# Forward substitution of 64x64 blocks on VectorE: spreading a finished row instead of gathering the rows above

## Chip, cores and metric

The kernel runs on one core of one Trainium2 chip. The metric is the device time of one execution in microseconds (us). The kernel before was run three times: 2924.29 us is the median, 2923.99 and 2924.81 the ends.

## The reference, cut to what matters

One inference step of a one-layer hybrid decoder over 1024 prompt positions and 32 sample positions: a SwiGLU feed-forward block, a layer norm, one wide projection that feeds two mixers in parallel (a gated spatial MLP and a gated DeltaNet), a merge, a layer norm, and a second feed-forward block. The DeltaNet mixer works in chunks of 64 positions with 8 heads. For each chunk and head it needs the inverse of a unit lower triangular 64x64 matrix:

```python
a_mat = jnp.where(strict, jnp.einsum('nbhid,nbhjd->nbhij', kb, k) * decay, 0.0)
eye = jnp.eye(L, dtype=q.dtype)
t_inv = lax.linalg.triangular_solve(eye + a_mat, jnp.broadcast_to(eye, a_mat.shape),
                                    left_side=True, lower=True, unit_diagonal=True)
u_vals = jnp.einsum('nbhij,nbhjv->nbhiv', t_inv, v * beta[..., None])
w_vals = jnp.einsum('nbhij,nbhjd->nbhid', t_inv, kb * jnp.exp(G)[..., None])
```

The prompt has 16 chunks and 8 heads, so there are 128 such matrices: one on each of the 128 partitions.

## The kernel before

TensorE does the large products in float32 split into a high and a low part, three matmuls for each product, in "unit pieces": `unit_piece` makes one 128x352 output from 8 weight tiles, 24 matmuls (lines 387 to 389). There are three pieces, one for each third of the positions, for each 128 columns of a weight. Everything else (convolutions, norms, DeltaNet, sampling) is a Python generator in a "lane".

The order of the instructions is laid out by a planner inside the kernel while it is built. It keeps `self.pet`, the time at which TensorE would be, and for VectorE, ScalarE and GpSimd an `Engine` object (line 151) that charges each instruction a fixed part plus a part for each element of a partition: 0.10 us and 1.04 ns on VectorE (`Core`, line 174), 0.12 us and 2.2 ns on GpSimd. A charge begins at the later of the engine's own planned end and `cur`, the planned end of the instruction issued just before in the same lane step, whichever engine that was on. `tick` runs after each three matmuls of a piece and lets each lane that is due go on by one step (line 335). `drain(g)` (line 356) lets planned time run until generator `g` is finished; no matmul of a unit piece is issued during a drain. `tt` (line 304) puts an elementwise instruction on GpSimd or VectorE, whichever would end first by the plan, with a bonus for GpSimd. Each engine then executes its own instructions in the order in which they were issued.

The work around the change is in `mixer` (line 1718). Unit pieces for k, q and v run first; their convolutions and transposes are generators that use VectorE heavily. `solve_gen` (line 1243) begins when all eight heads of k are done. It loads A, the 128 negated strictly lower triangular matrices, into `sA` (64x64 on each partition, row i and column j), and sets `sT` to the identity, held as `T[c, i]`: column c first, so that one column of the inverse is contiguous. For each row i from 1 to 63 it multiplies the columns found so far by row i of A (`prod`, tile `sP` or `sQ`) and sums over the inner index (`fold`, a tensor_reduce) into `T[:, i]`. Columns go in groups of 16, which leaves out much of the zero triangle. For i over 32 one of the products goes to GpSimd where the plan has it free. After each step, `ahead()` holds the generator as long as VectorE's planned end is over 0.8 us ahead of TensorE.

When the solve is done, four ScalarE copies write the transposed inverse back into `sA`, and two DMAs on SyncE's queue write `sT` and `sA` to memory. `comb_gen` (line 1295), eight in one lane, loads parts of them for each head and combines two 64x64 blocks into a 128x128 block with the `px` matmuls.

Beside the solve, in order of issue, there are z pieces, four units of gate pieces ("ga"), and two `sample_gen` (line 1448), one after the other in one lane. A sample generator has a chain of small steps over TensorE, VectorE and ScalarE, and ends with four rounds in which `spread` (line 1575) makes a tile `km`, TensorE makes 8 products `su` from it, and VectorE adds these to the states `s`. Line 1815 drains the second one, then adds the eight `comb_gen`. The gv pieces and further gate pieces follow, then lines 1843 to 1845 drain the solve, the spatial gate's norm (`gvln_gen`, lane "ln") and the last `comb_gen`, before the u pieces.

Of the kernel before, what the change touches and what calls it, by code (L numbers as in the profile page):

```python
# [12 lines left out]
F32 = mybir.dt.float32  # L13
# [3 lines left out]
ALU = mybir.AluOpType  # L17
AX = mybir.AxisListType
# [3 lines left out]
P = 128  # L22
# [239 lines left out]
class Kern:  # L262
# [979 lines left out]

    def solve_gen(self):

        nc = self.nc
        v = nc.vector
        while self.kdone < 8:
            yield 1.0
        yield 4.0
        Ab, Tb = self.big("sA", 4096), self.big("sT", 4096)  # L1250
        nc.sync.dma_start(Ab, self.scNd.rearrange("h s n i j -> (h s n) (i j)"))
        nc.gpsimd.memset(Tb, 0.0)
        nc.gpsimd.memset(Tb[:, 0:4096:65], 1.0)
        A, T = Ab.rearrange("p (i j) -> p i j", j=64), Tb.rearrange("p (c j) -> p c j", j=64)
        yield 8.0
        cost = 0.0
        m0, m1 = self.row("sP", F32, 1024), self.row("sQ", F32, 1024)

        def prod(e, i, c0, o, m):
            n, w = min(16, i - c0), i - c0  # L1260
            x = m[:, o:o + n * w].rearrange("p (c j) -> p c j", j=w)
            e.tensor_tensor(out=x, in0=T[:, c0:c0 + n, c0:i], in1=A[:, i, c0:i].unsqueeze(1).to_broadcast([P, n, w]), op=ALU.mult)
            return c0, n, x

        def fold(i, c0, n, x):
            v.tensor_reduce(out=T[:, c0:c0 + n, i:i + 1].rearrange("p c j -> p (c j)"), in_=x, axis=AX.X, op=ALU.add)
        def ahead():
            return v.end > self.pet + 0.8
        for i in range(1, 64):
            b1 = prod(nc.gpsimd if i > 32 and nc.gpsimd.end < self.pet + 0.3 else v, i, 16, 0, m1) if i > 16 else None  # L1270
            b0 = prod(v, i, 0, 0, m0)
            while ahead():
                yield -1.0
            fold(i, *b0)
            while ahead():
                yield -1.0
            late = [prod(v, i, c0, o, m0) for c0, o in ((32, 0), (48, 512)) if i > c0]
            while ahead():
                yield -1.0
            for b in late:  # L1280
                fold(i, *b)
            while ahead():
                yield -1.0
            if b1:
                fold(i, *b1)
            while ahead():
                yield -1.0
        for s in range(4):
            nc.scalar.copy(A[:, s * 16:(s + 1) * 16, :], T[:, :, s * 16:(s + 1) * 16].rearrange("p c j -> p j c"))
            yield  # L1290
        nc.sync.dma_start(self.scT, Tb)
        nc.sync.dma_start(self.scTn, Ab)
        self.solved = True
# [905 lines left out]
```

## Time and profile before

| | before |
| --- | --- |
| median of three runs | 2924.29 us |
| profiled execution | 2927.93 us |
| its span, first to last instruction | 2926.2 us |
| TensorE busy | 2763.6 us, 94% of the span |
| VectorE busy | 1811.3 us, 62% |
| ScalarE busy | 1111.8 us, 38% |
| GpSimd busy | 1473.4 us, 50% |
| mean granted TensorE clock | 0.970 of full speed |

The engines are named PE (TensorE matmuls), PEld (its weight loads), DVE (VectorE), ACT (ScalarE), POOL (GpSimd) and SP (SyncE). Nearly all elementwise instructions are recorded under line 167, the call in `Engine`, so they are told apart by the names of their tiles. Matmuls are pipelined: a busy share of PE near 100% does not say that it is at its peak, and a granted clock under 1.00 stretches the same matmuls. Idle time is put down to what ended it.

### The profile page before, as it was taken

The page shows a single profiled execution, that of the slowest core. Times are in us where ns is not written, and L with a number is a line of the kernel's source. Part 1 is how long each engine was busy: PE and PEld are TensorE (multiplying, and loading weights), DVE is VectorE, ACT ScalarE, POOL GpSimd, SP SyncE. Part 2 cuts the span into 40 slices and gives each one's busy share as a digit, 9 for nine tenths or more (in the row PEclk, how much of TensorE's full clock was granted, in tenths as well). Part 3 has the DMA queues.
Part 4 walks back from the last instruction along what each step waited for, and adds up shares of the span by engine and source line. Part 5 has one row for each costly group of instructions (what it writes and reads, how often), then busy time and mean ns, then how long its engine had stood idle before and what let it go on. Part 6 is the DMA issues. An engine that isn't in the chain of part 4 may idle for free.

```text
span 2926.2 us, 44704 instructions
## 1 busy us (share of the span) xinstructions
PE 2763.6 (94%) x17467; PEld 2716.2 (93%) x17467; DVE 1811.3 (62%) x2859; ACT 1111.8 (38%) x2216; POOL 1473.4 (50%) x867
## 2 busy tenths in 40 slices
PE   9998999999899998998999999999989989999995
PEld 8998899999789998998999999999989988999995
DVE  4646655455768999999363445036785466554556
ACT  4433333333345654321632433224443333333332
POOL 6656866665435452445233123232466568666653
PEclk9999999999899999998999999999999999999997
DMA  6442222221238995442444278475333422212211
GB/s 232 138 144 87 92 65 66 87 75 56 74 92 155 204 189 118 119 137 77 130 131 159 86 250 280 142 258 191 126 116 133 140 84 93 73 62 83 80 51 40
DMA packets 236867, 359.41 MB, mean 123 GB/s; under 512 B 72144, under 2 KB 169040, under 8 KB 236272
## 3 DMA queue, kind: packets, MB, share of 16 engines
q1 hardware_dynamic: 236656, 356.55, 40.1%
q8 instruction: 137, 2.24, 0.3%
q14 instruction: 74, 0.61, 0.1%
HBM read 279.59 MB, written 76.91 MB: 122 GB/s over the span
## 4 chain that ended last, share of the span: by engine, by line
PE 67%; DVE 17%; issue 6%; POOL 5%; ACT 2%; DMA 2%; SPq 0%; POOLq 0%; DVEq 0%; ACTq 0%
PE ps L387 16%; PE ps L389 15%; PE ps L388 15%; PE A L387 3%; PE A L389 3%; PE A L388 3%; DVE v L167 2%; DVE k L167 2%; DVE m L167 1%; POOL s L167 1%; PE F L387 1%; PE F L389 1%; PE F L388 1%; DVE q L167 1%; POOL wl L167 1%
## 5 line engine op out<-in xcount | busy, mean ns | idle before, releaser
L167 POOL TENSOR_TENSOR wl<-w,wh 128x1024 fp32r<-128x1024 f32 x217 | 546.6, 2529 | 768.9 <-ACT wh L167 591.2
L387 PE MATMUL ps<-x1h,wh 128*128 128x352 f32 x1536 | 515.2, 335 | 1.8 <-ACT wh L167 1.1
L389 PE MATMUL ps<-x1h,wl 128*128 128x352 f32 x1536 | 497.4, 324 | 1.8 <-POOL wl L167 1.8
L388 PE MATMUL ps<-x1l,wh 128*128 128x352 f32 x1536 | 497.9, 324 | 0.0
L387 PE MATMUL ps<-h,wh 128*128 128x352 f32 x1056 | 344.7, 326 | 18.3 <-DVE m L167 9.0
L389 PE MATMUL ps<-h,wl 128*128 128x352 f32 x1056 | 343.4, 325 | 6.5 <-POOL wl L167 6.5
L167 POOL TENSOR_TENSOR s<-w,s 128x512 fp32r<-128x512 f32 x158 | 217.7, 1390 | 194.8 <-ACT s L167 194.1
L387 PEld LDWEIGHTS ps<-x1h,wh 128*128 128x128 f32 x1536 | 293.3, 191 | 6.8 <-issue 1.4
L389 PEld LDWEIGHTS ps<-x1h,wl 128*128 128x128 f32 x1536 | 292.4, 190 | 2.1 <-POOL wl L167 2.1
L388 PEld LDWEIGHTS ps<-x1l,wh 128*128 128x128 f32 x1536 | 293.7, 191 | 0.1
L167 ACT CAST wh<-w 128x1024 fp32r<-128x1024 f32 (+1 forms) x257 | 263.6, 1044 | 75.7 <-PE ps L388 45.1
L388 PE MATMUL ps<-h,wh 128*128 128x352 f32 x704 | 228.0, 324 | 1.0 <-DVE h L167 1.0
L387 PEld LDWEIGHTS ps<-h,wh 128*128 128x128 f32 x1056 | 199.6, 189 | 20.9 <-DVE m L167 9.9
L389 PEld LDWEIGHTS ps<-h,wl 128*128 128x128 f32 x1056 | 200.0, 189 | 8.0 <-POOL wl L167 7.9
L167 ACT CAST s<-w 128x512 fp32r<-128x512 f32 x220 | 130.9, 618 | 167.7 <-DVE w L167 69.9
L387 PE MATMUL A<-T,s 128*128 128x352 f32 x528 | 176.7, 335 | 17.3 <-ACT T L167 10.6
L388 PE MATMUL A<-T,s 128*128 128x352 f32 x528 | 173.7, 329 | 0.5 <-DVE T L167 0.5
L389 PE MATMUL A<-T,s 128*128 128x352 f32 x528 | 173.5, 329 | 0.0
L167 DVE TENSOR_TENSOR p<-p,B 128x352 f32<-128x352 f32 x44 | 22.8, 519 | 235.0 <-PE B L389 235.0
L167 DVE SCALAR_TENSOR_TENSOR m<-ps,m 128x352 f32<-128x352 f32 x264 | 125.5, 515 | 32.6 <-PE ps L389 32.3
L167 DVE SCALAR_TENSOR_TENSOR acc<-ps,acc 128x352 f32<-128x352 f32 x264 | 125.7, 515 | 31.9 <-PE ps L389 31.6
L388 PEld LDWEIGHTS ps<-h,wh 128*128 128x128 f32 x704 | 132.9, 189 | 1.5 <-DVE h L167 1.5
(481 smaller groups left out, 7293.2 us busy)
## 6 DMA issues: line engine op xcount, KB each, us to landing
w<-in_wu SPq DMA_DIRECT2D x176, 512.0 KB
w<-in_wd SPq DMA_DIRECT2D x88, 512.0 KB
w<-in_wm SPq DMA_DIRECT2D x64, 512.0 KB
w<-in_wo SPq DMA_DIRECT2D x24, 512.0 KB
acc<-in_xt SPq DMA_DIRECT2D x12, 352.0 KB
scr_x<-acc SPq DMA_DIRECT2D x12, 352.0 KB
scr_z<-z SPq DMA_DIRECT2D x24, 176.0 KB
scr_ga<-tg SPq DMA_DIRECT2D x24, 176.0 KB
```

What stands on the lines that cost most here:

```text
L167: return f(*a, **kw)
L387: nc.tensor.matmul(ps[:, :C], lh, xh, start=(start and i == 0), stop=False, skip_group_check=not start)
L388: nc.tensor.matmul(ps[:, :C], lh, xl, start=False, stop=False, skip_group_check=not start)
L389: nc.tensor.matmul(ps[:, :C], ll, xh, start=False, stop=(i == n - 1), skip_group_check=not start)
```

## The change

For each j from 0 to 62, row j of the inverse is finished; it is multiplied by column j of A below the diagonal, for all columns c up to j and all rows i below j in one instruction, and a second instruction adds the products onto `T`. So 63 pairs of VectorE instructions take the place of the products and folds. No part goes to GpSimd, tile `sQ` is gone, and the planner is asked only once for each j, after the pair, whether VectorE is too far ahead. The work before the loop (load, memsets) and behind it (four copies, two stores) is the same.

```diff
-        cost = 0.0
-        m0, m1 = self.row("sP", F32, 1024), self.row("sQ", F32, 1024)
-
-        def prod(e, i, c0, o, m):
-            n, w = min(16, i - c0), i - c0
-            x = m[:, o:o + n * w].rearrange("p (c j) -> p c j", j=w)
-            e.tensor_tensor(out=x, in0=T[:, c0:c0 + n, c0:i], in1=A[:, i, c0:i].unsqueeze(1).to_broadcast([P, n, w]), op=ALU.mult)
-            return c0, n, x
-
-        def fold(i, c0, n, x):
-            v.tensor_reduce(out=T[:, c0:c0 + n, i:i + 1].rearrange("p c j -> p (c j)"), in_=x, axis=AX.X, op=ALU.add)
-        def ahead():
-            return v.end > self.pet + 0.8
-        for i in range(1, 64):
-            b1 = prod(nc.gpsimd if i > 32 and nc.gpsimd.end < self.pet + 0.3 else v, i, 16, 0, m1) if i > 16 else None
-            b0 = prod(v, i, 0, 0, m0)
-            while ahead():
-                yield -1.0
-            fold(i, *b0)
...
-            late = [prod(v, i, c0, o, m0) for c0, o in ((32, 0), (48, 512)) if i > c0]
...
-            for b in late:
-                fold(i, *b)
...
-            if b1:
-                fold(i, *b1)
-            while ahead():
+        m = self.row("sP", F32, 1024)
+        for j in range(63):
+
+            n, w = j + 1, 63 - j
+            x = m[:, 0:n * w].rearrange("p (c i) -> p c i", i=w)
+            t = T[:, 0:n, j + 1:64]
+            v.tensor_tensor(out=x, in0=T[:, 0:n, j:j + 1].to_broadcast([P, n, w]), in1=A[:, j + 1:64, j].unsqueeze(1).to_broadcast([P, n, w]),
+                            op=ALU.mult)
+            v.tensor_tensor(out=t, in0=t, in1=x, op=ALU.add)
+            while v.end > self.pet + 0.8:
                 yield -1.0
```

## Rows read from the trace of the kernel before

**Rows 1.** The page of the profile: busy time of DVE and PE in 40 equal slices of the span (73 us each), in tenths.

```profile
PE   9998999999899998998999999999989989999995
DVE  4646655455768999999363445036785466554556
```

**Rows 2.** Busy time of each engine in five stretches around the solve. Columns: stretch in us, its length, then PE, PEld, DVE, ACT and POOL busy us (instructions), granted PE clock, DMA share, GB/s.

```profile
1060.00:1190.00 130.00, 114.55 (x710) 113.08 (x709) 127.81 (x192) 57.86 (x125) 44.83 (x17) 0.92 0.65 122
1190.00:1345.00 155.00, 154.20 (x1037) 145.31 (x1037) 142.65 (x289) 43.15 (x103) 74.49 (x61) 1.00 0.35 118
1345.00:1405.00 60.00, 50.49 (x288) 49.13 (x286) 56.92 (x101) 16.63 (x44) 28.55 (x12) 0.80 0.21 71
1420.00:1435.00 15.00, 10.25 (x63) 9.78 (x62) 2.83 (x6) 6.87 (x19) 2.86 (x2) 0.77 0.57 176
1540.00:1560.00 20.00, 16.68 (x104) 15.85 (x103) 10.18 (x9) 3.67 (x6) 5.32 (x7) 0.83 0.64 186
```

**Rows 3.** The same for the instructions that touch `sT` alone, in the first three of these stretches. Columns: stretch, length, then DVE, ACT and POOL busy us (instructions), clock, DMA share, GB/s.

```profile
1060.00:1190.00 130.00, 34.80 (x95) 0.00 (x0) 0.00 (x0) 0.92 0.65 122
1190.00:1345.00 155.00, 90.24 (x149) 0.00 (x0) 26.28 (x15) 1.00 0.35 118
1345.00:1405.00 60.00, 40.06 (x48) 0.14 (x1) 11.24 (x5) 0.80 0.21 71
sum 345.00, DVE 165.10 ACT 0.14 POOL 37.52; mean DVE 55.03 ACT 0.04 POOL 12.51
```

**Rows 4.** What PE waited for: the first row from 1060 to 1190 us, the next from 1345 to 1405 us, the last from the whole span (both of its waits lie between 1420 and 1560 us). Columns: total us, times, longest us.

```profile
PE ta L1106 <- DVE v L167: 15.3, 4, 5.8
PE su L1609 <- POOL km L167: 6.4, 2, 3.3
PE spt L1598 <- DVE ons L167: 1.9, 1, 1.9
PE ta L1106 <- DVE gt L167: 1.3, 1, 1.3
...
PE px L1313 <- DMA tn<-scr_N: 8.1, 2, 4.8
```

**Rows 5.** The instructions that write or read `sT`: line, engine, operation, out<-in and count; ns min/median/max; first and last start in us; the first shapes.

```profile
L167 DVE TENSOR_TENSOR sP<-sT,sA x109: 147/550/3208, 1065.9 to 1400.4; 128x1 f32<-128x1 f32 x3, 128x4 f32<-128x4 f32 x3, 128x9 f32<-128x9 f32 x3, 128x16 f32<-128x16 f32 x3
L167 DVE TENSOR_REDUCE sT<-sP x109: 143/489/1189, 1066.1 to 1401.3; 128x1 f32<-128x1 f32 x3, 128x2 f32<-128x4 f32 x3, 128x3 f32<-128x9 f32 x3, 128x4 f32<-128x16 f32 x3
L167 DVE TENSOR_REDUCE sT<-sQ x47: 144/533/921, 1106.3 to 1402.4; 128x1 f32<-128x1 f32 x1, 128x2 f32<-128x4 f32 x1, 128x3 f32<-128x9 f32 x1, 128x4 f32<-128x16 f32 x1
L167 DVE TENSOR_TENSOR sQ<-sT,sA x27: 149/427/2330, 1105.4 to 1385.0; 128x1 f32<-128x1 f32 x1, 128x4 f32<-128x4 f32 x1, 128x9 f32<-128x9 f32 x1, 128x16 f32<-128x16 f32 x1
L167 POOL TENSOR_TENSOR sQ<-sT,sA x20: 1236/1778/3187, 1190.6 to 1392.7; 128x272 f32<-128x272 f32 x1, 128x288 f32<-128x288 f32 x1, 128x336 f32<-128x336 f32 x1, 128x352 f32<-128x352 f32 x1
L167 ACT COPY sA<-sT x4: 2024/2039/2048, 1404.9 to 1416.0; 128x1024 f32<-128x1024 f32 x4
```

**Rows 6.** Single products of the solve on DVE, in order of time: start us, us, line, operation, out<-in, shapes. The first product of row i has 16 times i elements once i is over 16.

```profile
1187.30 0.69 DVE L167 TENSOR_TENSOR sP<-sT,sA 128x512 f32<-128x512 f32 x1
...
1258.28 0.92 DVE L167 TENSOR_TENSOR sP<-sT,sA 128x736 f32<-128x736 f32 x1
...
1267.15 2.63 DVE L167 TENSOR_TENSOR sP<-sT,sA 128x752 f32<-128x752 f32 x1
...
1339.09 1.64 DVE L167 TENSOR_TENSOR sP<-sT,sA 128x912 f32<-128x912 f32 x1
...
1394.83 1.19 DVE L167 TENSOR_TENSOR sP<-sT,sA 128x1008 f32<-128x1008 f32 x1
```

**Rows 7.** Instructions by group with their shapes: one large ACT cast with contiguous reading; a DVE copy that reads 64 elements 32 bytes apart and a DVE instruction over 72 contiguous elements; a DVE product that reads one of its inputs 32 bytes apart, 8 elements, and its contiguous neighbour. Columns of the first four: count, busy us, mean ns, idle before; of the last: ns min/median/max, first and last start.

```profile
L167 ACT CAST wh<-w 128x1024 fp32r<-128x1024 f32 x26 | 27.2, 1045 | 0.0
...
L167 DVE TENSOR_SCALAR beta<-bt 128x72 f32<-128x72 f32 x1 | 0.2, 197 | 0.3 <-ACT bt L167 0.3
L167 DVE COPY gc<-g 128x64 f32<-128x64 f32 x1 | 0.2, 196 | 0.0
...
L167 DVE TENSOR_TENSOR brk<-beta,rk 128x8 f32<-128x8 f32 x1 | 0.2, 168 | 0.0
...
L167 DVE TENSOR_TENSOR ot<-oy x30: 151/166/404, 1253.0 to 1821.4; 128x8 f32<-128x8 f32 x24, 32x4 f32<-32x4 f32 x6
```

**Rows 8.** The end of the second sample generator in order of time: start us, us, engine, line, operation, out<-in, shapes, and in brackets the idle time before and what ended it. First PE, then POOL. Some records of one kind that follow each other are merged into one row.

```profile
1344.89 0.32 PE L389 MATMUL ps<-x1h,wl 128*128 128x352 f32 x1
...
1353.49 7.19 PE L1609 MATMUL su<-kS,km 64*128 64x128 f32 x32 [3.34 <-POOL km L167]
1363.70 3.78 PE L1609 MATMUL su<-kS,km 64*128 64x128 f32 x16 [3.02 <-POOL km L167]
1367.41 0.66 PE L387 MATMUL ps<-x1h,wh 128*128 128x352 f32 x1
...
1349.16 2.42 POOL L167 TENSOR_TENSOR sQ<-sT,sA 128x672 f32<-128x672 f32 x1 [2.14 <-DVE sT L167]
1351.55 4.09 POOL L167 TENSOR_TENSOR km<-kv,cst 64x1024 f32<-64x1024 f32 x2
1359.32 2.48 POOL L167 TENSOR_TENSOR sQ<-sT,sA 128x688 f32<-128x688 f32 x1 [3.69 <-DVE sT L167]
1361.76 1.89 POOL L167 TENSOR_TENSOR km<-kv,cst 64x1024 f32<-64x1024 f32 x1
```

More of the change, by code (lines that the diff above doesn't have):

```diff
@@ L1255, in solve_gen @@
         yield 8.0
-        cost = 0.0
-        m0, m1 = self.row("sP", F32, 1024), self.row("sQ", F32, 1024)
-        def prod(e, i, c0, o, m):
-            n, w = min(16, i - c0), i - c0
-            x = m[:, o:o + n * w].rearrange("p (c j) -> p c j", j=w)
-            e.tensor_tensor(out=x, in0=T[:, c0:c0 + n, c0:i], in1=A[:, i, c0:i].unsqueeze(1).to_broadcast([P, n, w]), op=ALU.mult)
-            return c0, n, x
-        def fold(i, c0, n, x):
-            v.tensor_reduce(out=T[:, c0:c0 + n, i:i + 1].rearrange("p c j -> p (c j)"), in_=x, axis=AX.X, op=ALU.add)
-        def ahead():
-            return v.end > self.pet + 0.8
-        for i in range(1, 64):
-            b1 = prod(nc.gpsimd if i > 32 and nc.gpsimd.end < self.pet + 0.3 else v, i, 16, 0, m1) if i > 16 else None
-            b0 = prod(v, i, 0, 0, m0)
-            while ahead():
-                yield -1.0
-            fold(i, *b0)
-            while ahead():
-                yield -1.0
-            late = [prod(v, i, c0, o, m0) for c0, o in ((32, 0), (48, 512)) if i > c0]
-            while ahead():
-                yield -1.0
-            for b in late:
-                fold(i, *b)
-            while ahead():
-                yield -1.0
-            if b1:
-                fold(i, *b1)
-            while ahead():
+        m = self.row("sP", F32, 1024)
[7 more added lines that the diff above has]
+            while v.end > self.pet + 0.8:
                 yield -1.0
```

## The prediction

> **What bounds the kernel now.** I read four things, in this order. The slices first [rows 1]: PE is busy at 8 or 9 tenths throughout, so PE sets the time, and only what makes PE wait or run at a lower clock can move it. DVE is full in slices 14 to 19, roughly 950 to 1400 us, and the solve lies in the last three quarters of that. So I cut this part into stages and look at each for lost PE time, which I define as idle time plus busy time multiplied by what the clock is short of 1.00 [rows 2]:
>
> - 1060 to 1190 us: 15.5 idle + 0.08 x 114.6 = 24.6 us lost. DVE is busy for 127.8 of 130 us. PE waits for convolved v tiles from DVE [rows 4].
> - 1190 to 1345 us: 0.8 us lost. DVE is busy for 142.7 of 155 us, but PE needs little of it at once.
> - 1345 to 1405 us: 9.5 + 0.20 x 50.5 = 19.6 us lost. This holds the drain of the second sample generator, with waits for `km` from POOL [rows 4].
> - 1420 to 1435 us: 4.8 + 0.23 x 10.3 = 7.1 us lost. PE waits for the first `tn` load of the block combination [rows 4].
> - 1540 to 1560 us: 3.3 + 0.17 x 16.7 = 6.2 us lost, again behind a `tn` load, for the last head but one.
>
> Third, the waits that name the releaser [rows 4]. Last, what the solve takes in each stage [rows 3]: 34.8, 90.2 and 40.1 us of DVE, 165.1 in all, and 37.5 us of POOL.
>
> **What the change removes and adds on DVE.** Removed are 109 + 27 products and 109 + 47 reductions on DVE, 292 instructions and 165.1 us, and 20 products on POOL, 37.5 us [rows 3, 5]. A product of 1 element takes 147 ns at the least and one of 1008 takes 1.19 us [rows 5, 6], so an undisturbed instruction is 0.146 us plus 1.04 ns an element. The 736-element product agrees (0.92 us, worked out 0.91). The old reductions have 57,440 elements by the loop's sizes: 156 x 0.146 + 57,440 x 0.00104 = 82.5 us. That leaves 82.6 us for 136 products, with some 47,000 elements (57,440 less about 20 x 520 on POOL): 19.9 + 48.9 = 68.8 us undisturbed. The rest, 13.8 us or 0.10 us each, is disturbance, as in the 752-element product that took 2.63 us [rows 6].
>
> Added are 126 instructions. Their elements are the sum of (j+1)(63-j), 43,680, twice. Undisturbed: 126 x 0.146 + 87,360 x 0.00104 = 109.3 us. All of them have two inputs as the old products have, so I add 0.10 us each: **122 us**, 43 less than now.
>
> The one new thing is how the new product reads A. Old products read a row of A, contiguous; the new one reads a column, elements 256 bytes apart. No DVE row of the trace reads that far apart. The bounds are these. ScalarE's copy of `sT` does, and takes 2.04 us for 1024 elements [rows 5] where a contiguous cast takes 1.045 [rows 7]: 0.97 ns more an element, which on 43,680 elements would be 42 us, and the solve 164 us, no gain at all. On DVE itself, reading 32 bytes apart costs nothing that can be seen: 64 elements in 196 ns against 72 contiguous ones in 197, and a product of 8 at 168 ns against a median of 166 [rows 7]. I take no price, by the rows of the same engine, and keep 42 us as the other end. Below zero is excluded, since no contiguous row is faster per element than the fit.
>
> [...]
>
> **What it does to the plan.** The plan decides how early the solve ends. By its charges (0.10 us plus 1.04 ns an element) the old DVE part is 137.9 us: 28.9 for rows 1 to 32, 75.5 for rows 33 to 56, 33.5 for the rest. Row 32 is reached at 1187 us and row 57 at 1339 us [rows 6]. The new loop charges 103.5 us in all. If the plan hands out DVE time at the same pace, the new loop has had 28.1 by 1190 us (j = 20) and needs 75.4 more, just what was handed out between 1190 and 1345 us. The GpSimd products also push VectorE's planned end, as the charge of the next product begins at their end; that goes, so I expect the solve to end at **1325 to 1345 us** instead of 1402, before the drain. The real DVE time per charge stays about the same: 90.2 / 75.5 = 1.20 now, and 122 / 103.5 = 1.18 after. So neither of the first two stages changes by itself.
>
> **The sum on PE.**
>
> - 1060 to 1190 us: the solve takes 34.8 us of DVE now [rows 3]; the new pairs up to j = 20 take 42 x 0.246 + 22,946 x 0.00104 = 34.2. Zero, with 5 either way for other order.
> - 1190 to 1345 us: nothing to win [rows 2]; DVE's cover stays at about 92%. Zero.
> - The drain: PE has no piece to work on between 1345.2 and 1367.4 us [rows 8]. Twice a `km` on POOL stands behind a `sQ` product that itself waited for DVE, and `su` waits 3.34 and 3.02 us for it. With the solve done, the four `km` (2.0 us each) follow each other, and I work out a resumption some 8 us earlier. What comes late next is the chain of small sample steps itself, which PE still has to sit out; if the longer pairs hold some of those back (third case below), part is lost. I take **-5** (0 to -10).
> - 1380 to 1405 us: the wait for `gt` behind DVE, 1.3 us [rows 4]: **-1**.
> - 1420 to 1435 us: the copies and stores of the solve end before the first `comb_gen` is even added, so its load finds its data written: **-7**. What else could be late is the load itself, but the later heads' loads are covered by pieces.
> - 1540 to 1560 us: with `comb_gen` some 30 us earlier, the drains before the u pieces hold only the norm, whose instructions are not TensorE's: **-5** of 6.2.
>
> Sum -18 us, on the profiled execution's 2927.9 us. That one is 3.6 us above the median of the runs, so I put the median at 2924.3 - 18 = **2906 us**. The 43 us of DVE and 37 us of POOL are mostly not gained, as PE had cover for them in the second stage. The four copies, two stores, the load and the memsets are unchanged. The tile `sQ` that is no longer taken frees one row buffer, which I cost at nothing: no wait for a row buffer stands among PE's [rows 4].
>
> **The rivals.**
>
> *The column read is slow on DVE* (ends slower). For it speaks the ScalarE row; against it the DVE rows at 32 bytes. The plan knows nothing of it, so it packs the same 103.5 us of charges, and they run at 164. In the first stage DVE is the limit: 11,473 elements up to j = 20 x 0.97 ns = 11 us straight onto PE. After that 32,207 x 0.97 = 31 us, of which 155 - 143 = 12 us find room on DVE [rows 2] and 19 don't. +30 - 18 = +12, **2936 us**. It turns slower than before when the read costs more than 0.69 ns an element (11.5 + 32.2 of them at that price are 18 + 12 us).
>
> *The sample chain gets later.* At its longest a pair charges 2 x (0.10 + 1.06) = 2.3 us between two looks at the plan, an old step about half of that. A sample step on VectorE queues behind it: some 20 such steps in the two generators x 0.6 us = 12 us later, and the drain is longer by as much. -18 + 12 = -6, **2918 us**. For it: the generators run one after the other, and the solve runs all through the first. Against: the old loop's GpSimd products also push VectorE's planned end by over a microsecond.
>
> *The first stage gains too.* Fewer, undisturbed instructions let DVE catch up there, and half of the 24.6 us goes: -18 - 12, **2894 us**. Little speaks for it, since the plan fills whatever is free.
>
> **How the numbers follow.** The forecast has 0.53, the slow column read 0.27, the later sample chain 0.15, the gain in the first stage 0.05. A measurement of this kernel can tell about 0.2%, 6 us, from no change. Forecast: 0.48 faster, 0.05 within. Slow read: 0.01 faster, 0.05 within, 0.21 slower. Later chain: 0.06 faster, 0.08 within, 0.01 slower. First stage: 0.05 faster. That makes 0.60 faster, 0.18 within 0.2%, 0.22 slower. The forecast's own range is 2893 to 2918 us. Down to 2890 and up to 2938 us, half of the slow read's chance and a little below are left out, under 2 in 10.
>
> **What would show it.** Right: 126 DVE instructions of the solve with 105 to 135 us in all; a 1024-element product at about 1.21 us where it is not disturbed, equal to the add behind it; the last one before 1345 us; no wait of `px` for `tn`; PE back on pieces within 14 us of the drain's begin; the first stage about as long. Wrong: products at about twice the time of the adds, PE losing time between 1190 and 1345 us, the solve ending in or after the drain, or a drain longer than 22 us.

## The result: 1% slower

| | before | after |
| --- | --- | --- |
| median of the runs beside each other | 2924.55 us | 2957.44 us |
| ratio, 95% interval | | 1.0105 [1.0093, 1.0117] |
| profiled execution | 2927.93 us | 2954.28 us |
| DVE in the solve | 165.1 us, 292 instructions | 173.3 us, 126 instructions |
| POOL in the solve's products | 37.5 us | 0 |
| end of the last DVE instruction of the solve | about 1403 us | about 1359 us |

The forecast was 2906 us and the range ended at 2938 us. DVE gained nothing, and PE lost 33 us. First the solve's instructions after the change, in the view that lists what writes or reads `sT` (before the change: [rows 5]):

```profile
L167 DVE TENSOR_TENSOR sP<-sT,sA x63: 261/1670/4129, 1064.2 to 1358.0; 128x63 f32<-128x63 f32 x2, 128x124 f32<-128x124 f32 x2, 128x183 f32<-128x183 f32 x2, 128x240 f32<-128x240 f32 x2
L167 DVE TENSOR_TENSOR sT<-sT,sP x63: 223/1049/3273, 1064.5 to 1358.3; 128x63 f32<-128x63 f32 x2, 128x124 f32<-128x124 f32 x2, 128x183 f32<-128x183 f32 x2, 128x240 f32<-128x240 f32 x2
```

Product and sum have the same sizes, yet the medians are 1670 and 1049 ns. The largest pair in the order of time on DVE (start us, us), against the 1008-element product of [rows 6]:

```profile
1239.54 2.03 DVE L167 TENSOR_TENSOR sP<-sT,sA 128x1024 f32<-128x1024 f32 x1
1241.61 1.23 DVE L167 TENSOR_TENSOR sT<-sT,sP 128x1024 f32<-128x1024 f32 x1
```

So the product that reads a column takes 0.80 us longer than the sum beside it, 0.78 ns for each of 1024 elements.

The stretches of [rows 2] no longer lie at the same times, so I cut the time by the work of PE, at the moments when ScalarE takes the result of a unit piece: first and last z piece, last gate piece before the drain, first and last gelu piece behind it (`gx`; the span to the last one takes in the combination and the norm). The rows are ScalarE's, with first and last start; before, then after:

```profile
L167 ACT ACTIVATE z<-ps,prm x24: 543/554/558, 1171.3 to 1285.5; 128x352 f32<-128x352 f32 x24
...
1345.30 0.55 ACT L167 ACTIVATE tg<-ps,hb 128x352 f32<-128x352 f32 x1 [1.94 <-POOL tg L167]
...
L167 ACT ACTIVATE gx<-ps,prm x48: 528/554/557, 1373.9 to 1695.5; 128x352 f32<-128x352 f32 x48
```

```profile
L167 ACT ACTIVATE z<-ps,prm x24: 529/554/558, 1174.0 to 1314.4; 128x352 f32<-128x352 f32 x24
...
1386.77 0.55 ACT L167 ACTIVATE tg<-ps,hb 128x352 f32<-128x352 f32 x1 [11.92 <-PE ps L389]
...
L167 ACT ACTIVATE gx<-ps,prm x48: 554/555/558, 1421.2 to 1727.6; 128x352 f32<-128x352 f32 x48
```

PE is 2.7 us late at the first z piece, 28.9 at the last, 41.5 at the last gate piece, 47.3 at the first gelu piece, and 32.1 at the last one. So the z stage lost 26.2 us, the gate stage 12.6, the drain 5.8, and the stretch behind it won 15.2. Behind that, the profiled execution lies 6 us nearer to the one before; no run here says why. The next rows are busy times (columns as in [rows 2]): the kernel before from 1174 to 1315 us, then the changed kernel in the same stretch, which is its z stage, and in its drain.

```profile
1174.00:1315.00 141.00, 140.03 (x924) 133.30 (x922) 132.96 (x258) 43.95 (x98) 61.54 (x53) 1.00 0.40 128
```

```profile
1174.00:1315.00 141.00, 114.12 (x697) 109.53 (x696) 137.41 (x145) 37.86 (x82) 37.47 (x21) 0.88 0.28 85
...
1389.00:1415.00 26.00, 14.97 (x73) 14.44 (x71) 17.33 (x43) 2.32 (x9) 10.29 (x7) 0.56 0.06 14
```

After the change DVE is busy for 137.4 of 141 us, while PE idles for 26.9 and has a mean granted clock of 0.88: PE now waits for DVE there. What is behind it, these rows don't say; the experiments do. What PE waited for from 1060 to 1700 us (columns as in [rows 4]):

```profile
PE ta L1106 <- DVE v L167: 29.3, 6, 11.8
PE spt L1578 <- DVE ons L167: 21.0, 2, 11.0
PE snt L1502 <- DVE Ds L167: 8.1, 1, 8.1
PE ps L387 <- DVE s L167: 2.1, 1, 2.1
```

`spt` and `snt` are tiles of the sample chain. In the same stretch of the kernel before, `ta` on `v` took 15.7 us and `spt` 2.4. The waits of `px` for `tn` and of `su` for `km` are gone, as forecast.

### The profile page after: what moved, and what is told of

The parts are those of the page before. It is cut to its first block, busy times and chain, and to the rows that moved or that the text cites. A ratio compares the mean times of both kernels' runs of the same rounds, so it can differ in the third digit from the quotient of the medians.

```text
span 2952.5 us, 44507 instructions
## 1 busy us (share of the span) xinstructions
PE 2762.7 (94%) x17467; PEld 2716.6 (92%) x17467; DVE 1805.1 (61%) x2691; ACT 1114.1 (38%) x2216; POOL 1452.9 (49%) x849
## 4 chain that ended last, share of the span: by engine, by line
PE 40%; DVE 5%; issue 3%; POOL 3%; ACT 1%; DMA 0%; POOLq 0%; SPq 0%; DVEq 0%; ACTq 0%
PE ps L387 10%; PE ps L389 9%; PE ps L388 9%; PE A L387 2%; PE A L389 1%; PE A L388 1%; DVE m L167 1%; PE ma L1326 1%; POOL s L167 1%; POOL m L167 1%; PE F L387 1%; PE F L389 1%; PE F L388 1%; POOL wl L167 1%; DVE vt L167 1%
## 5 line engine op out<-in xcount | busy, mean ns | idle before, releaser
L167 POOL TENSOR_TENSOR wl<-w,wh 128x1024 fp32r<-128x1024 f32 x219 | 557.6, 2556 | 899.4 <-ACT wh L167 597.4
```

What stands on the lines that cost most here:

```text
L167: return f(*a, **kw)
```

## The experiments

Theory 1: the column read costs DVE time that the plan doesn't know of, and PE pays. Theory 2: the planner is asked once for a pair that it charges with up to 2.3 us, so the sample chain is planned late and the drain gets long, whatever a product costs. All ratios are to the kernel before.

How early the chain runs I tell by `skS`, a tile that each of the two sample generators fills on PE midway in its chain: the number of unit pieces, from the first z piece on, that ScalarE had begun to take before the first `skS` matmul. There are 36 pieces, 24 of z and 12 of gates, before the drain.

**The inverse held row by row.** Element `A[i, j]` is now read once and repeated over a contiguous run of n columns; the order on PE is unchanged.

```diff
-            x = m[:, 0:n * w].rearrange("p (c i) -> p c i", i=w)
-            t = T[:, 0:n, j + 1:64]
-            v.tensor_tensor(out=x, in0=T[:, 0:n, j:j + 1].to_broadcast([P, n, w]), in1=A[:, j + 1:64, j].unsqueeze(1).to_broadcast([P, n, w]),
+            x = m[:, 0:n * w].rearrange("p (i c) -> p i c", c=n)
+            t = T[:, j + 1:64, 0:n]
+            v.tensor_tensor(out=x, in0=T[:, j:j + 1, 0:n].to_broadcast([P, w, n]), in1=A[:, j + 1:64, j:j + 1].to_broadcast([P, w, n]),
...
-        nc.sync.dma_start(self.scT, Tb)
-        nc.sync.dma_start(self.scTn, Ab)
+        nc.sync.dma_start(self.scTn, Tb)
+        nc.sync.dma_start(self.scT, Ab)
```

> The spread loop with the inverse held row by row (row index first), so that a product reads one element of A's column and repeats it over a contiguous run; the same instructions in the same order, the same plan charges, the same PE order, and the two stores at the end exchange their targets. Theory 1 (the column read costs DVE 0.8 ns an element that the plan does not know, and PE pays for it): a 1024-element product falls from 2.03 to about 1.22 us, the solve from 173 to about 130 us of DVE, and the time to 2905 to 2920 us. Theory 2 (the pairs are long between two looks at the plan, so the sample chain is planned late, whatever a product costs): the time stays within 10 us of the changed kernel's 2957 us.

Measured: 2927.96 us, ratio 1.0004 [0.9994, 1.0013]. The solve takes 137.1 us of DVE; its largest pair, in the order of time:

```profile
1223.50 1.21 DVE L167 TENSOR_TENSOR sP<-sT,sA 128x1024 f32<-128x1024 f32 x1
1224.74 1.22 DVE L167 TENSOR_TENSOR sT<-sT,sP 128x1024 f32<-128x1024 f32 x1
```

Theory 1 is shown: with as many instructions of the same sizes, the same plan charges and the same order on PE, 29.5 us come back. But the time is 8 us above what theory 1 alone allowed. The drain from 1357 to 1392 us is as long as in the changed kernel.

**The plan told the price of the column read.**

```diff
             v.tensor_tensor(out=x, in0=T[:, 0:n, j:j + 1].to_broadcast([P, n, w]), in1=A[:, j + 1:64, j].unsqueeze(1).to_broadcast([P, n, w]),
                             op=ALU.mult)
+            v.end += n * w * 0.79e-3
+            self.cur = v.end
             v.tensor_tensor(out=t, in0=t, in1=x, op=ALU.add)
```

> The changed kernel with the plan told the price: VectorE's planned end is moved on by 0.79 ns for each element of a product. The same DVE work as the changed kernel, 173 us. Theory 1 in the form that the plan's ignorance is what costs: PE's idle time between 1190 and 1345 us falls from some 30 to under 10 us, the solve ends later than 1358 us, near 1390 to 1400 us, and the time is 2920 to 2935 us. If the DVE time itself costs, wherever it is put: 2950 us or more. Theory 2: slower than the changed kernel or the same, since the planned pairs are longer still, 2955 to 2975 us.

Measured: 2941.04 us, ratio 1.0048 [1.0033, 1.0063]. It lies between the theories' numbers, 16 us under the changed kernel. The z stage is back to 114.0 us as before the change, so what PE lost there was due to the plan's ignorance. PE's idle time between 1190 and 1345 us is 8.5 us, where the changed kernel has 24.5; but the solve ends at 1375 us, not near 1390 to 1400 as expected. The drain grows to 54.1 us: a pair is now planned at up to 3.1 us, and the chain is later still (18 pieces in place of 16). Each theory has one half of this run.

**A second look at the plan, row layout.** The edit against the row layout with one look:

```diff
                             op=ALU.mult)
+            while v.end > self.pet + 0.8:
+                yield -1.0
             v.tensor_tensor(out=t, in0=t, in1=x, op=ALU.add)
```

> The row-by-row layout with a second look at the plan, between the product and the sum. Theory 1: within 6 us of the row-by-row layout with one look, since the price of the read is gone in both. Theory 2: 15 to 30 us faster than with one look, as the chain of sample steps no longer queues behind 2.3 us.

Measured: **2903.75 us, ratio 0.9922 [0.9905, 0.9939]**, 24 us under the row layout with one look, as theory 2 says. It beats both kernels. Its ScalarE rows, cut as above:

```profile
L167 ACT ACTIVATE z<-ps,prm x24: 542/554/557, 1170.9 to 1286.0; 128x352 f32<-128x352 f32 x24
...
1350.92 0.55 ACT L167 ACTIVATE tg<-ps,hb 128x352 f32<-128x352 f32 x1 [5.47 <-PE ps L389]
...
L167 ACT ACTIVATE gx<-ps,prm x48: 553/554/557, 1360.7 to 1671.7; 128x352 f32<-128x352 f32 x48
```

From the last gate piece to the first gelu piece it is 9.8 us, where the row layout with one look has 34.4 and the kernel before 28.6. Against one look, the drain gives 24.6 us and the z stage 8.4; the stretch behind the drain and the time before the first z piece give 4.4 and 3.2 of it back.

**The column read put into the old loop.**

```diff
-            e.tensor_tensor(out=x, in0=T[:, c0:c0 + n, c0:i], in1=A[:, i, c0:i].unsqueeze(1).to_broadcast([P, n, w]), op=ALU.mult)
+            y = A[:, c0:i, i] if e is v else A[:, i, c0:i]
+            e.tensor_tensor(out=x, in0=T[:, c0:c0 + n, c0:i], in1=y.unsqueeze(1).to_broadcast([P, n, w]), op=ALU.mult)
```

> The kernel before, but its products on DVE read a column of A in place of a row (the upper triangle holds zeros, so what is solved is not the inverse); the instructions, their order and the plan are the same. Theory 1: about 47,000 elements at 0.8 ns are 37 us more on DVE that the plan does not know, PE waits for them mostly between 1060 and 1345 us, and the time is 2945 to 2965 us. Theory 2: within 8 us of the kernel before, 2917 to 2933 us.

Measured: 2957.6 us, ratio 1.0104 [1.0089, 1.0119]; the solve takes 209.3 us of DVE, 44.2 more. The read alone does as much harm in the old loop as the whole change did. The sample chain stands where it stood (13 pieces). The price shows at small sizes too. The products of 64 and 81 elements by their shapes (columns: count, busy us, mean ns, idle before), the kernel before first:

```profile
L167 DVE TENSOR_TENSOR sP<-sT,sA 128x81 f32<-128x81 f32 x1 | 0.2, 232 | 0.0
L167 DVE TENSOR_TENSOR sP<-sT,sA 128x64 f32<-128x64 f32 x1 | 0.2, 224 | 0.0
```

```profile
L167 DVE TENSOR_TENSOR sP<-sT,sA 128x81 f32<-128x81 f32 x1 | 0.3, 301 | 0.0
L167 DVE TENSOR_TENSOR sP<-sT,sA 128x64 f32<-128x64 f32 x1 | 0.3, 269 | 0.0
```

**Column read and two looks.** The second look as above, in the changed kernel.

> The changed kernel, column read kept, with a second look at the plan between the product and the sum. If the column read (about 29 us so far) and the single look (about 24 us so far) add up: 2957 - 24 = 2933 us, between 2925 and 2940. If the second look is worth something only where the products are cheap, because DVE is too far behind in any case: 2945 to 2957 us. The first sample generator's skS should then stand behind 12 to 13 unit pieces, not 16.

Measured: 2937.32 us, ratio 1.0033 [1.0024, 1.0043]. The second look is worth 20 us here and 24 in the row layout; the read costs 29.5 us with one look and 33.6 with two. The two causes add, within 4 us.

**Half pairs, one look behind each.**

```diff
-            n, w = j + 1, 63 - j
+            w = 63 - j
+            for c0, c1 in ((0, (j + 2) // 2), ((j + 2) // 2, j + 1)):
+                n = c1 - c0
...
+                x = m[:, 0:n * w].rearrange("p (i c) -> p i c", c=n)
+                t = T[:, j + 1:64, c0:c1]
```

> The row-by-row layout with each pair cut into two pairs over half of the columns, one look at the plan behind each: 252 instructions in place of 126, the longest planned stretch between two looks 1.3 us in place of 2.3. If the length between two looks is what makes the sample chain late: skS behind 12 to 13 pieces, drain under 15 us, and 2904 us plus up to 10 for 126 more instructions of 0.15 us, 2903 to 2917 us. If it is the place of the second look (between product and sum) that helps: like the row-by-row layout with one look or slower, 2925 to 2940 us.

Measured: 2926.32 us, ratio 0.9997 [0.9987, 1.0007]. Neither branch holds in full. The chain is early (the first skS behind 12 pieces), so a look between product and sum is not needed for it: short pieces do it as well. But the time is in the range of the other branch. The solve takes 161.2 us of DVE in 250 instructions, 31 us more than with two looks and whole columns, where I had reckoned 19; the second skS stands one piece later than with two looks (31, not 30), and the drain is 19.7 us.

**A tighter limit.** In the row layout with two looks, 0.2 in place of 0.8 in both conditions.

> The row-by-row layout with two looks, and the solve held as long as VectorE's planned end is over 0.2 us ahead of TensorE, not 0.8. If what is queued in front of the sample steps decides: the chain comes still earlier and the solve ends later, past the drain's begin (1351 us) or near it; 2895 to 2908 us. If the solve's end decides instead: it ends after the drain, the combination's first load is waited for again (7 us), and the time is 2908 to 2920 us.

Measured: 2915.39 us, ratio 0.9956 [0.994, 0.9973]: the time of the second branch, but not by the wait that it named. The drain falls to 7.8 us, but the solve ends at 1372 us, behind the drain's begin at 1354, and the first `px` starts at 1392 where it started at 1367. The load `tn` is waited for 1.7 us, not 7 (3.0 us with the limit of 0.8). What PE waits for in that stretch is `gt` on DVE, 10.0 us.

**One look in the old loop.** Four of the five conditions for each row are taken out.

```diff
             b0 = prod(v, i, 0, 0, m0)
-            while ahead():
-                yield -1.0
             fold(i, *b0)
-            while ahead():
-                yield -1.0
...
```

> The kernel before with one look at the plan for each row i, at its end, in place of five; products, sums, sizes and reads unchanged. If the length between two looks makes the sample chain late in the old loop too: skS behind 16 pieces or more in place of 13, a longer drain, and 2940 to 2960 us. If only the spread loop is sensitive: 2918 to 2932 us.

Measured: 2946.97 us, ratio 1.0063 [1.0047, 1.0079]. The first skS stands behind 15 pieces (16 expected), the drain is 59.1 us long. What PE waited for from 1050 to 1700 us:

```profile
PE snt L1514 <- DVE Ds L167: 19.6, 2, 18.2
PE ta L1106 <- DVE v L167: 14.2, 4, 9.0
PE spt L1590 <- DVE ons L167: 9.1, 2, 7.2
PE stt L1549 <- DVE Ds L167: 7.7, 2, 7.5
```

For three of these four PE waits in the sample chain. Theory 2 holds in the old loop as well, in direction. Its longest row is charged with about 5 us by its sizes, a pair with 2.3; yet the first skS is one piece earlier than in the spread loop with one look, and the second one later (36, not 35). So the longest piece alone doesn't give the lateness.

**The read by itself.** Behind the solve of the row layout with two looks, for s = 1, 2, 3, 4, 8, 16, 32, 64:

```diff
+        for s in (1, 2, 3, 4, 8, 16, 32, 64):
...
+            src = Ab[:, 0:63 * s + 1:s].unsqueeze(1).to_broadcast([P, 16, 64])
+            for _ in range(3):
+                v.tensor_tensor(out=y, in0=m[:, 0:1024].rearrange("p (r x) -> p r x", x=64), in1=src, op=ALU.mult)
+                nc.scalar.copy(z, src)
```

> The row-by-row layout with two looks, with 24 products on DVE and 24 copies on ScalarE added behind the solve, three of each for every distance of 4, 8, 12, 16, 32, 64, 128 and 256 bytes between the elements read (64 of them, repeated 16 times, 1024 in all; nothing reads their result). The prediction went by two rows at 32 bytes, which showed no price on DVE. If the price is one of the large distance: products at 32 bytes take 1.22 us like those at 4, and only 128 or 256 bytes take 2.0. If those two rows were too short to show it: 2.0 us from 16 bytes on. If the second input of a product is not like a copy, ScalarE's copies step up (1.04 to 2.04 us) elsewhere than the products. The time of the whole is not the question here.

Measured, each row three instructions of 1024 elements with ns min/median/max; the number in the tile's name is the distance in bytes, `v` is DVE and `s` is ScalarE:

```profile
L167 DVE TENSOR_TENSOR by4v<-sP,sA x3: 1219/1225/1227, 1332.5 to 1335.0; 128x1024 f32<-128x1024 f32 x3
L167 ACT COPY by4s<-sA x3: 1037/1049/1051, 1330.9 to 1333.1; 128x1024 f32<-128x1024 f32 x3
L167 DVE TENSOR_TENSOR by8v<-sP,sA x3: 1224/1224/1226, 1337.0 to 1339.5; 128x1024 f32<-128x1024 f32 x3
L167 ACT COPY by8s<-sA x3: 1120/1158/1165, 1335.9 to 1338.2; 128x1024 f32<-128x1024 f32 x3
L167 DVE TENSOR_TENSOR by12v<-sP,sA x3: 1714/1745/3753, 1340.6 to 1346.2; 128x1024 f32<-128x1024 f32 x3
L167 ACT COPY by12s<-sA x3: 1568/1582/1603, 1343.5 to 1346.8; 128x1024 f32<-128x1024 f32 x3
L167 DVE TENSOR_TENSOR by16v<-sP,sA x3: 2036/2043/2059, 1354.5 to 1358.6; 128x1024 f32<-128x1024 f32 x3
L167 ACT COPY by16s<-sA x3: 2003/2013/2017, 1348.7 to 1352.8; 128x1024 f32<-128x1024 f32 x3
L167 DVE TENSOR_TENSOR by32v<-sP,sA x3: 2086/2099/3625, 1361.0 to 1366.8; 128x1024 f32<-128x1024 f32 x3
L167 DVE TENSOR_TENSOR by256v<-sP,sA x3: 1881/1899/1901, 1387.3 to 1391.2; 128x1024 f32<-128x1024 f32 x3
```

On DVE the price begins at 12 bytes and is whole at 16: 1.22 (8 bytes), 1.75, 2.04 us. At 32 bytes it is 2.10, no less than at 256. So a 1024-element product pays at 32 bytes, as the second branch says, and ScalarE's copies step up over the same distances (1.16, 1.58, 2.01 us). The reason that this branch gave, that both rows of [rows 7] were too short, holds for the product of 8 elements alone, where 0.8 ns an element is 6 ns. On the copy of 64 elements it would be 50 ns, and a 64-element product in the old loop showed 45 (269 against 224). That copy was set beside another operation of 72 elements, as the rows have no contiguous copy of its size. Why it shows no price isn't known: no run measured DVE copies at several distances. The kernel with these additions took 2949.6 us, which says nothing of the change.

## Why the prediction was wrong

The table gives the median times (the kernel before, run again beside the others, had medians of 2924.6 to 2926.7 us), the lengths of the stages, cut as above (us), the unit pieces before the first `skS` matmul of each sample generator, and DVE's busy time in the solve (us). The pieces are counted, the lengths are differences of ScalarE's starts.

| kernel | time | z | gates | drain | behind | skS after pieces | DVE |
| --- | --- | --- | --- | --- | --- | --- | --- |
| before | 2924.6 | 114.2 | 59.8 | 28.6 | 321.6 | 13, 32 | 165.1 |
| after: column, one look | 2957.4 | 140.4 | 72.4 | 34.4 | 306.4 | 16, 35 | 173.3 |
| row, one look | 2928.0 | 123.5 | 66.1 | 34.4 | 306.6 | 16, 35 | 137.1 |
| column, plan told | 2941.0 | 114.0 | 67.8 | 54.1 | 306.8 | 18, 36 | 181.9 |
| column, two looks | 2937.3 | 129.1 | 75.0 | 9.7 | 311.3 | 12, 30 | 169.6 |
| row, two looks | 2903.8 | 115.1 | 64.9 | 9.8 | 311.0 | 12, 30 | 130.1 |
| row, half pairs | 2926.3 | 118.7 | 73.2 | 19.7 | 306.9 | 12, 31 | 161.2 |
| row, two looks, limit 0.2 | 2915.4 | 120.0 | 64.8 | 7.8 | 324.2 | 12, 29 | 130.2 |
| before, column read | 2957.6 | 123.4 | 68.0 | 30.4 | 329.3 | 13, 32 | 209.3 |
| before, one look | 2947.0 | 109.7 | 68.0 | 59.1 | 306.9 | 15, 36 | 168.6 |

The second `skS` orders the drain in all ten kernels: 7.8 us at 29 pieces, 9.7 and 9.8 at 30, 19.7 at 31, 28.6 and 30.4 at 32, 34.4 twice at 35, 54.1 and 59.1 at 36, where all pieces are used up. What the chain has not done when the pieces end, PE sits out in the drain.

**The cost on DVE.** The step that failed first: "I take no price, by the rows of the same engine, and keep 42 us as the other end." The price is 0.78 ns an element in the largest product and 0.83 over all, 36.1 us between the changed kernel and the row layout (173.3 - 137.1), near the bound taken from ScalarE (0.97). I weighed a copy of 64 and a product of 8 elements on the same engine above a row of 1024 on another. The product could have shown 6 ns of its 168, and the copy had no contiguous copy of its size beside it. The run with all distances shows the price by itself: 1024 elements took 1.22 us on DVE at 4 and at 8 bytes, 1.75 at 12 and 2.04 at 16. And not every contiguous row is as slow as the fit, as I had it where I excluded a price below zero: a TENSOR_SCALAR of the kernel before (`vtm`, 1024 elements) has a median of 0.81 us, where the fit gives 1.21.

The 122 us was also short by 15 in the row layout: disturbance is 137.1 - 109.3 = 27.8 us, 0.22 us an instruction, not the 0.10 of the old products. The 0.10 came from 165.1 us of busy time, in which stretches where two instructions overlap count once; the old instructions' durations add up to 174.6 us, which makes 0.17 a product. And it is no share of every instruction. In the row layout 13 of the 126 hold 25.6 of the 27.8 us, 1.6 to 2.3 us each, and every one of these runs while a two-input instruction is under way on GpSimd. The other 24 that overlap GpSimd work hold 1.2 us together, and the 89 that overlap none hold 1.0. One of the 13, and what GpSimd did meanwhile (start us, us):

```profile
1260.05 3.22 DVE L167 TENSOR_TENSOR sT<-sT,sP 128x960 f32<-128x960 f32 x1
...
1259.41 2.84 POOL L167 TENSOR_TENSOR wl<-w,wh 128x1024 fp32r<-128x1024 f32 x1 [23.07 <-ACT wh L167]
```

No run took GpSimd's work away, so that it is the cause is read from the overlap and not shown by an experiment.

**The end of the solve** was put at 1325 to 1345 us. It came at 1359 in the changed kernel, 14 us past that, with PE's work there 29 to 41 us late, but still ahead of the drain at 1387. In the row layout it came at 1326 and 1332, as said.

**The stages.** The first one was taken at zero and is 2.7 us. The second was taken at zero and holds the loss: 26.2 + 12.6 us. With the row layout and two looks it is 0.9 and 5.1 us, nearer to zero once both causes are gone. The stretch behind the drain was put at -12 with the two `tn` waits, and -1 for `gt`; it is -15.2, and these waits are gone. The drain was put at -5 and is +5.8. With two looks it is 18.8 us shorter than before, so the room I saw was there and more, but the plan with one look gives it away.

**The rivals.** Two of the three came true together; the third, a gain in the first stage, did not (2.7 us lost there). The slow column read was priced at +30 against the forecast and is 29.5 us; it is shown by one edit each way. That the numbers meet is partly luck: I had 11 us in the first stage and 19 behind, and against the row layout it is 6 us up to the first z piece and 23 behind that. The later sample chain was priced at +12 and is 24 us in the row layout, 20 with the column read: the first skS stands 3 pieces later than before, and the second too, so some 11 us of lateness, as reckoned, but against two looks it is 4 and 5 pieces, and the drain is 24.6 us longer. The failing step of the sum is that I gave each of these a chance as if the other were absent, and predicted the case with neither. By my own prices -18 + 30 + 12 is +24, 2948 us; measured is 2957. The version without either, the row layout with two looks, has the ratio 0.9922, 23 us under the runs of before beside it, where the forecast was 18. So the gain that I saw is there in a kernel that was not the one at hand. But that 23 is near 18 is partly luck as well: the drain gave 18.8 us where I had 5, from an earlier chain that I hadn't reckoned with, the stretch behind it gave 10.6 where I had 13, and the gate stage took 5.1 where I had nothing.

**What a microsecond on DVE costs.** Time that the plan doesn't know of is mostly paid by PE: 29.5 of 36.1 us (one look), 33.6 of 39.5 (two looks), 31 of 44.2 (old loop). The rest, 6 to 7 us in the spread loop and 13 in the old one, found room; I had put 12 us of room on a price of 42.

What stays open: why a 64-element DVE copy at 32 bytes shows no price, whether GpSimd's work is the cause of the disturbance, and by what rule the lateness of the chain follows from the length of the pieces.

## What to carry to other kernels

Before a loop is turned round, look at the innermost distance of every operand: on DVE and ScalarE here, 1024 fp32 elements 16 bytes or more apart took 1.6 to 2 times as long as contiguous ones (1.90 to 2.10 us against 1.22, and 2.00 to 2.15 against 1.05), and choosing which index is innermost (here, holding the result by rows) removed that: 1.21 us again for the product.

Before a row is taken as evidence that something costs nothing, work out what it would show if the cost were there, and set it beside a row of the same operation and size.

In background work that is interleaved by a plan, the length of the piece between two looks at the plan is a cost of its own, separate from the work.

Rivals that rest on different mechanisms are not alternatives: add them, and give a chance to their sum.

## What the runs showed of the hardware

For 1024 fp32 elements the step in reading cost lies between 8 bytes (1.22 us on VectorE, 1.16 on ScalarE) and 16, with 12 bytes in between (1.75 and 1.58). At 16 bytes the two take about the same, 2.04 and 2.01 us; at 4 bytes they take 1.22 and 1.05, so the step is larger on ScalarE. At 256 bytes VectorE took 1.90 us in the run with all distances and 2.03 in the changed kernel's largest product, so a difference to 32 bytes (2.10 us) isn't shown. I hadn't expected the step at all at 32 bytes, since a copy of 64 elements (196 ns) and a product of 8 (168 ns) showed none [rows 7]; for products of the solve 256 bytes apart it shows at 64 elements as well (269 ns against 224).

In the row layout with one look, 13 of the solve's 126 two-input instructions on VectorE took 1.6 to 2.3 us more than their size asks for, each beside a two-input instruction on GpSimd. The 89 that ran while GpSimd did nothing were 1.0 us over in all.
